# A decoder layer in split fp32: 69 to 73 seven-product k-pairs, and 50 of them with two weight sums made by accumulating DMAs

## The chip, the cores and the metric

The kernel runs on one core of one Trainium2 chip. The metric is the device time of one launch in microseconds (us), as the median of the runs. A core has a matrix engine (TensorE, PE in the profile, with its weight loads as PEld), VectorE (DVE), ScalarE (ACT), GpSimd (POOL), SyncE (SP, which issues most DMAs here) and 16 DMA engines. SBUF is the on-chip memory, PSUM holds the accumulators of PE, and the weights come from DRAM.

## The reference

One layer of a decoder on 256 tokens of width 2048, all in float32. Its work is some thirty products of a 256-row activation with a weight matrix:

```python
hn = rmsnorm(h, norm_mix_w)
q, k, v, g_ret, xr, yr, g_a, g_b = split(hn @ w_in)          # 2048 x 14336
ret_out = silu(g_ret) * groupnorm(retention(rotary(q), rotary(k), v))
rnn_out = gelu(yr) * rg_lru(causal_dwconv(xr))
merged = sigmoid(g_a) * (ret_out @ w_proj_ret) + sigmoid(g_b) * (rnn_out @ w_proj_rnn)
h = h + merged @ w_mix_out
h = h + memory_cross_attention(rmsnorm(h), rmsnorm(mem), xa_w_q, xa_w_k, xa_w_v, xa_w_o)
up = causal_dwconv(rmsnorm(h) @ ffn_w_up)                    # 2048 x 11264
h = h + (silu(gate) * value) @ ffn_w_down                    # 5632 x 2048
return rmsnorm(h, final_norm_w)
```

## The kernel before

**Split products.** Every fp32 operand is split into a high part `hi` (a cast to float32r by ACT, line 446) and a rest `lo` (operand minus `hi`, by DVE, line 447). A product is three matmuls, `hi·hi`, `lo·hi` and `hi·lo` (`mm`, line 280), each 128 x 128 weights by 128 x 512 columns.

**The stream of weights.** `weight_plan` lists the 58 products in their order, and `weight_stream` cuts them into 358 chunks, which stand in DRAM in this order as `wall`. A chunk of a *pair* is one k-pair: two k-tiles of 128 rows by two column blocks of 512, four 128 x 512 tiles, 1 MB. `prefetch` (called by `chunks`) issues a chunk's load on SP, into one of three `raw` buffers, and its splits, two chunks ahead of PE; `hi` and `lo` tiles of 128 x 1024 rotate through six buffers each (`PART_BUFS`). The work that a chunk doesn't feed directly (convolutions, norms, transposes, token sums) is put in between by `later`, with distances in chunks that stand in the table `LAG`. The order on each engine is then made by a scheduler from these.

**Eight products or seven.** A plain k-pair multiplies two token halves by two k-tiles by two column blocks: eight products, 24 matmuls. A *seven-product* k-pair (`steps_pair`, the branch `if k2 in seven`) uses Strassen's scheme in Winograd's form on the 2 x 2 blocks: seven products, 21 matmuls. For it, seven weight tiles are split in place of four, and four weight sums are made first: `seven_parts` (line 468) makes them on DVE, with one add of 128 x 1024 and two of 128 x 512. Sums of the activations come from `sums_of`.

**Sums by DMA.** In the *loaded* kind, `load_twice` fetches one weight tile twice into the buffer `tw` (SP, 512 KB), `add_to` adds two other tiles to it straight from DRAM (POOL queue, line 325, 512 KB, `accum_op=ADD`), and `seven_loaded` (line 332) is left with two DVE adds of 128 x 512; its `raw` load is 768 KB. The *far* kind takes a subtraction from DVE: `request` fetches the weights early as `fr`, `subtract` writes their negative, rounded to float32r, with ACT (line 314), and a DMA on the POOL queue adds the weights themselves to it, which leaves the rest, `fl`; the `hi` cast of such weights is line 340.

**What sets kinds and places.** `MARKS` has one entry for each pair: `3` makes k-pair 3 a seven-product one, `23` a loaded one, `-4` makes k-pair 4 a plain one whose two halves are far, `-14` one with its first half far. `LAG` has the distances of early work, in chunks ahead of the chunk that needs it: `sum_load` and `sum_add` for the two DMAs of the loaded kind, `far_load` and `far` for `request` and `subtract`. `tw`, `fr` and `fl` take slots of the pool `bp`, 31 buffers of 4 KB a partition that also holds activations. The results of `ffn_w_down` are added to the residual rows by DMAs on the POOL queue (`nat<-o`, line 1302).

Of the kernel before, what the change touches and what calls it, by code (L numbers as in the profile page):

```python
# [28 lines left out]
BW = 512  # L29
KC = 4  # L30
KH = 2
# [3 lines left out]
WARM = 7  # L35
FREE = 300
LAG = dict(
    sums=3, two_heads=2, recur=3, gelu=6, merged=4, memory=1, memory_step=4, rnn=0, rnn_step=2,
    heads=6, heads_step=1, squares=4, squares_step=2, rows=17, rows_step=2, residual=2, gate=2,
    value=4, merge_turn=1, query_turn=2, key_turn=3, turn=3, attend=3, acc_m=0, acc_h=0,  # L40
    by_rotate=0, by_conv=0, by_gelu=1, by_attend=0, far=2, far_load=2, sum_load=4, sum_add=4,
)
EPS = 1e-6
GN_EPS = 1e-5
FF_PARTS = [4, 4, 3]
EARLY = [2, 2, 4, 4, 4]
MARKS = [
# [9 lines left out]
]  # L57

O_Q, O_K, O_V, O_G = 0, 1024, 2048, 4096
# [22 lines left out]
def both(w, c, row=0, nk=NT, apart=BW):  # L82

    return w, row, nk, (c, c + apart)


def weight_plan():

    plan = []
    for g in range(2):  # L90
        keys = [("w_in", 0, NT, c + g * BW) for c in (O_Q, O_K)]
        values = [("w_in", 0, NT, O_V + b * BW) for b in range(2)]
        first = [keys[0], values[0], both("w_in", O_K, apart=O_V + BW - O_K)]
        plan += keys + [both("w_in", O_V + 1024)] if g else first
        plan.append(both("w_in", O_G + g * 1024))
    for b in range(4):
        plan += [("w_in", 0, NT, c + b * BW) for c in (O_XR, O_YR)]
    plan += [("w_in", 0, NT, O_GB + b * BW) for b in range(2)] + [both("w_proj_rnn", 0)]
    plan += [both("w_in", O_GB + 1024), both("w_proj_rnn", 1024)]
    plan += [both(w, c + b * BW) for w, c in (("w_in", O_GA), ("w_proj_ret", 0)) for b in (0, 2)]  # L100
    plan += [both("w_mix_out", b * BW) for b in (0, 2)]
    plan += [both("xa_w_k", 0), both("xa_w_q", 0), both("xa_w_q", 2 * BW), both("xa_w_k", 2 * BW)]
    plan += [both(w, b * BW) for w in ("xa_w_v", "xa_w_o") for b in (0, 2)]
    for kind, *a in ff_plan():
        if kind == "down" and sum(a) < NF // 4:
            plan += [both("ffn_w_down", b * BW, a[0] * BW, 4 * a[1]) for b in (0, 2)]
        elif kind == "down":
            plan += [("ffn_w_down", a[0] * BW, 4 * a[1], b * BW) for b in range(4)]
        else:
            plan.append(both("ffn_w_up", a[0] * BW, apart=FF))  # L110
    marks, out = iter(one for stage in MARKS for one in stage), []
    for w, row, nk, c in plan:
        if isinstance(c, tuple):
            one = next(marks)
            seven, far = tuple(k % 10 for k in one if k > 0), tuple(-k for k in one if k < 0)
            loaded = tuple(k % 10 for k in one if k > 10)
            out += [(w, row, nk, (*c, seven, far, loaded))] if seven else [(w, row, nk, half) for half in c]
        else:
            out.append((w, row, nk, c))
    return out  # L120


def marks_of(w, row=0):

    return next((c[2] for one, r, _, c in weight_plan() if (one, r) == (w, row) and isinstance(c, tuple)), ())
# [19 lines left out]

def pieces(i, nk, c):

    sizes = EARLY if i < 2 else [KH] * (nk // KH) if isinstance(c, tuple) else [KC] * (nk // KC)
    return [(sum(sizes[:j]), n) for j, n in enumerate(sizes)]


def in_turn(products):

    return [c for o in products for c in o[:-1]] + [o[-1] for o in products]


def kind_of(c, k):

    if not isinstance(c, tuple):
        return c  # L160
    k2 = k // KH
    kinds = (k2 in c[4], k2 in c[2], k2 in c[3], k2 + 10 in c[3], True)
    return (*c[:2], (4, 1, 2, 3, 0)[kinds.index(True)])


def weight_stream():

    out = [
        [(w, row + k * P, n, kind_of(c, k)) for k, n in pieces(i, nk, c)]
        for i, (w, row, nk, c) in enumerate(weight_plan())  # L170
    ]
    out[:2] = [[one for pair in zip(*out[:2]) for one in pair]]
    out[-4:-1] = [in_turn(out[-4:-1])]
    return [one for chunks in out for one in chunks]


# [18 lines left out]
def hybrid_layer(  # L195
# [17 lines left out]
    act, dve, pe, pool, sp = nc.scalar, nc.vector, nc.tensor, nc.gpsimd, nc.sync  # L213
# [21 lines left out]
    def acc():  # L235
        return pm.tile([P, 2, BW], F32, tag="acc", name=nm("acc"))
# [46 lines left out]
    plan = weight_plan()  # L283
# [9 lines left out]
    at, scale0, split, far = [0], [], [], {}  # L293
# [202 lines left out]
    def ended(steps):  # L496

        for a in steps:
            pass
        return a  # L500
# [34 lines left out]
    def gemm_n(*args):  # L535
        return ended(steps_n(*args))
# [384 lines left out]
    for g in range(2):  # L921
        dec = big([P, 4, S], s="dec")
        vs, turned = [], ([], [])
        for b, o in enumerate((O_Q, O_K)):
# [6 lines left out]
            if b and not g and paired():  # L931
                a, v = pair("w_in", 0, xs, NT, O_K, O_V + BW)
                scaled(a, rs0)
                by_dma(a, rotate_both)
            else:
                a = gemm_n("w_in", 0, xs, NT, o + g * BW) if g + b else q0
                turned_rows(a, rs0, rotate_both, 2 - b if g + b else 3, g + b > 0, LAG["by_rotate"])
            if b == 1:
                sp.dma_start(
                    out=dec,  # L940
# [47 lines left out]
    rnn = []  # L988
# [91 lines left out]
    merged, rsms, hrow = [], [], []  # L1080
# [222 lines left out]

    def down_final(b0, hid, n):

        steps = [steps_n("ffn_w_down", b0 * BW, hid, n, b * BW) for b in range(3)]
        for st in steps:
            for _ in range(n // KC - 1):
                next(st)
        for b, st in enumerate(steps):  # L1310
            h = hrow[b]
            dve.tensor_add(h, h, ended(st))
            finish(b)
        last_down(b0, hid, n, 3)
# [55 lines left out]
    def finish(b):  # L1370

        for tt in range(2):
            y = hrow[b][:, tt, :]
            square(y, ss3[:, tt, b : b + 1])
            dve.tensor_tensor(out=y, in0=y, in1=wfin[b // 2][:, b % 2, :], op=ALU.mult)
# [30 lines left out]
    hid = {}  # L1406
    for kind, b, *n in ff_plan():
        if kind == "up":
            b0 = max(one[1] for one in ff_plan() if one[0] == "down" and one[1] <= b)
            used = marks_of("ffn_w_down", b0 * BW) if b0 < sum(FF_PARTS[:2]) else ()  # L1410
            seven = tuple(i - 2 * (b - b0) for i in used)
            up(b, hid.setdefault(b, []), seven, LAG["value"] if b < NF // 4 - 1 else 3)
        else:
            final = b + n[0] == NF // 4
            if final:
                wfin = []
                for i in range(2):
                    t = big([P, 2, BW], s="wf")
                    sp.dma_start(
                        out=t.rearrange("p a n -> p (a n)"),  # L1420
                        in_=final_norm_w[i * 1024 : (i + 1) * 1024].partition_broadcast(P),
                    )
                    wfin.append(t)
            (down_final if final else down)(b, Hidden(hid, b), 4 * n[0])
# [38 lines left out]
```

## Time and profile before

| | us |
|---|---|
| runs | 1957.58, 1960.05, 1960.06 |
| median | 1960.05 |
| the profiled execution's own time | 1958.17 |
| its span, first to last instruction | 1956.4 |
| PE busy in the span | 1945.4 |
| DVE busy | 1670.9 |
| ACT busy | 1444.6 |
| POOL busy | 49.3 |

The profile is of one execution. Busy time is the time in which an engine had an instruction in work; matmuls overlap, so the busy time of PE says whether it ran, not how fast. A group of instructions is shown by line, engine, operation and tiles, with its count, its busy time, the mean of one, and the idle time ahead of it with what ended it. The chain of waits is followed back from the last instruction. A row of the timeline has the start, the time taken, the instruction, and in brackets the idle time before it. Rows on stretches (windows) give the busy time of each engine in a stretch, the granted clock, the share of time in which the 16 DMA engines were busy, and what they moved.

### The profile page before, as it was taken

How to read it: one execution, taken by the hardware profiler on the slowest of the kernel's cores; microseconds unless marked ns; L12 is line 12 of the kernel's file. 1: busy time of each engine (PE TensorE's matmuls, PEld its weight loads, DVE VectorE, ACT ScalarE, POOL GpSimd, SP SyncE). 2: the span in 40 equal slices, each digit the busy share in tenths (PEclk: the TensorE clock that was granted, in tenths of full speed). 3: DMA queues.
4: the chain of work that ended last, by engine and by line, in shares of the span. 5: the costliest groups of instructions: out<-in, count | busy, mean ns of one | idle time of the engine just before them, and what ended most of it. 6: DMA issues, size and time to landing. Idle time of an engine off the chain costs nothing.

```text
span 1956.4 us, 24194 instructions
## 1 busy us (share of the span) xinstructions
PE 1945.4 (99%) x8747; PEld 1616.2 (83%) x8747; DVE 1670.9 (85%) x2160; ACT 1444.6 (74%) x1774; POOL 49.3 (3%) x48
## 2 busy tenths in 40 slices
PE   9999999999999999999999999999999999999998
PEld 7888888888888888888888888888888888888887
DVE  6897986788999898887888767889999989999986
ACT  6666758999655676778678777888887578874784
POOL 0000000010000000000000000000000000000000
PEclk9999999999999999999999999999999999999999
DMA  8757667766567576778766666676677667768673
GB/s 331 239 202 203 221 227 206 223 209 211 180 226 250 183 269 215 268 241 263 237 212 219 213 190 192 210 253 224 212 231 230 239 223 233 231 198 264 228 234 130
DMA packets 202456, 438.74 MB, mean 224 GB/s; under 512 B 142560, under 2 KB 147168, under 8 KB 158560
## 3 DMA queue, kind: packets, MB, share of 16 engines
q1 hardware_dynamic: 199024, 425.14, 65.3%
q0 software_dynamic: 3312, 12.06, 3.2%
q8 instruction: 68, 1.11, 0.2%
q14 instruction: 52, 0.43, 0.1%
HBM read 391.54 MB, written 2.10 MB: 201 GB/s over the span
## 4 chain that ended last, share of the span: by engine, by line
PE 88%; DVE 6%; ACT 2%; issue 2%; DMA 2%; POOL 0%; SPq 0%; POOLq 0%; DVEq 0%; ACTq 0%
PE acc L280 62%; PE sm L280 26%; DVE lo L447 2%; DMA raw<-in_wall 1%; ACT hi L446 1%; DVE fv L1277 1%; DVE o L622 0%; DVE raw L468 0%; ACT f L672 0%; DVE o L633 0%; DVE s L697 0%; DVE fo L1286 0%; DVE fg L1277 0%; ACT pl L659 0%; ACT fg L1275 0%
## 5 line engine op out<-in xcount | busy, mean ns | idle before, releaser
L447 DVE TENSOR_TENSOR lo<-raw,hi 128x1024 fp32r<-128x1024 f32 (+1 forms) x837 | 963.1, 1178 | 192.4 <-ACT hi L446 185.0
L280 PE MATMUL acc<-hi,s 128*128 128x512 f32 (+1 forms) x3534 | 1083.7, 388 | 1.9 <-ACT hi L446 0.8
L446 ACT CAST hi<-raw 128x1024 fp32r<-128x1024 f32 (+1 forms) x837 | 816.6, 1010 | 327.0 <-DVE raw L468 86.3
L280 PEld LDWEIGHTS acc<-hi,s 128*128 128x128 f32 x3534 | 660.9, 188 | 137.6 <-ACT hi L446 1.3
L280 PE MATMUL acc<-lo,s 128*128 128x512 f32 (+1 forms) x1743 | 676.2, 388 | 0.0
L280 PE MATMUL sm<-hi,s 128*128 128x512 f32 x1496 | 460.9, 389 | 0.0
L280 PEld LDWEIGHTS acc<-lo,s 128*128 128x128 f32 x1743 | 327.5, 188 | 68.2 <-DVE lo L447 1.3
L280 PEld LDWEIGHTS sm<-hi,s 128*128 128x128 f32 x1496 | 280.9, 188 | 58.2 <-ACT prob L1198 0.2
L280 PE MATMUL sm<-lo,s 128*128 128x512 f32 x728 | 283.6, 390 | 0.2 <-DVE lo L447 0.2
L672 ACT COPY f<-pt 128x1024 uint16<-128x1024 uint16 x128 | 167.2, 1354 | 12.2 <-DMA pt<-pl 12.2
L468 DVE TENSOR_TENSOR raw<-raw 128x512 f32<-128x512 f32 (+1 forms) x195 | 169.0, 867 | 2.6
L280 PEld LDWEIGHTS sm<-lo,s 128*128 128x128 f32 x728 | 136.7, 188 | 29.1 <-DVE lo L447 0.8
L280 PE MATMUL acc<-hi,ts 128*128 128x512 f32 x414 | 127.5, 389 | 0.0
L280 PEld LDWEIGHTS acc<-hi,ts 128*128 128x128 f32 x414 | 77.8, 188 | 16.1
L280 PE MATMUL acc<-lo,ts 128*128 128x512 f32 x207 | 80.8, 391 | 0.7 <-DVE lo L447 0.7
L659 ACT COPY pl<-o 128x1024 uint16<-128x1024 uint16 x64 | 62.7, 1040 | 2.9 <-DVE o L633 2.8
L659 ACT COPY pl<-rows 128x1024 uint16<-128x1024 uint16 x44 | 43.8, 1043 | 16.2 <-DVE rows L689 16.2
L1403 ACT ACTIVATE o<-o,ro 128x512 f32<-128x512 f32 x44 | 30.3, 718 | 31.1 <-DVE o L633 30.9
L633 DVE TENSOR_TENSOR o<-o,sm 128x512 f32<-128x512 f32 x64 | 42.6, 684 | 5.6 <-PE sm L280 5.5
L280 PEld LDWEIGHTS acc<-lo,ts 128*128 128x128 f32 x207 | 38.9, 188 | 9.5 <-DVE lo L447 1.5
L1277 DVE SCALAR_TENSOR_TENSOR fg<-f,pf,fg 128x255 f32<-128x255 f32 (+1 forms) x88 | 40.3, 480 | 4.6 <-ACT fg L1275 4.1
L622 DVE TENSOR_TENSOR o<-o,acc 128x512 f32<-128x512 f32 x64 | 43.7, 683 | 0.5
(197 smaller groups left out, 1196.2 us busy)
## 6 DMA issues: line engine op xcount, KB each, us to landing
raw<-in_wall SPq DMA_DIRECT2D x342, 1024.0 KB, 4.9
fr<-in_wall SPq DMA_DIRECT2D x11, 512.0 KB, 6.5
fl<-fr POOLq DMA_DIRECT2D x11, 512.0 KB, 9.0
raw<-in_wall SPq DMA_DIRECT2D x8, 512.0 KB, 7.3
nat<-in_x SPq DMA_DIRECT2D x8, 512.0 KB, 9.9
nat<-o POOLq DMA_DIRECT2D x8, 512.0 KB, 6.6
raw<-in_wall SPq DMA_DIRECT2D x4, 768.0 KB, 4.3
pt<-pl SPq DMA_TRANSPOSE x128, 3.5
```

The costliest lines, as they stand in the source:

```text
L280: tc.keep_in_program_order(pe.matmul(*a, **k))
L446: act.copy(hi[:, cs], src[:, cs])
L447: dve.tensor_tensor(out=lo[:, cs], in0=src[:, cs], in1=hi[:, cs].bitcast(F32), op=ALU.subtract)
L468: dve.tensor_tensor(out=o, in0=a, in1=b, op=ALU.add)
L622: dve.tensor_tensor(out=o, in0=a, in1=b, op=op)
L633: dve.tensor_tensor(out=o, in0=o, in1=a, op=ALU.add)
L659: act.copy(planes[:, tt], words[:, tt])
L672: act.copy(halves_[:, :, :, cs], turned_[:, :, :, cs])
L1277: dve.scalar_tensor_tensor(out=y[:, s:S], in0=z[:, j, 0 : S - s], scalar=pf[:, 2 - s, t : t + 1], in1=y[:, s:S], op0=ALU.mult, op1=ALU.add,)
L1403: act.mul(a[:, tt, :], a[:, tt, :], rs2[:, tt : tt + 1])
```

## The change

It rewrites two tables. `MARKS` now has 73 seven-product k-pairs for 69, and 50 of them are loaded for 4; the twelve halves that are far stood at eleven. All 32 seven-product k-pairs of the feed-forward (31 before) are loaded, where two were. The four that are new are in the second pair of the `w_in` columns of `g_a`, in the first pairs of `xa_w_v` and `xa_w_o`, and in the seventh block of `ffn_w_up`. `LAG` moves some of the early work: the accumulating DMA of a loaded k-pair is issued, in program order, with its chunk (`sum_add` 4 to 0), the negation and DMA of a far one with its chunk too (`far` 2 to 0), and a few tasks shift by one to four chunks (`two_heads`, `rnn`, `heads`, `squares`, `residual`). `by_attend` gives eight scalings of 128 x 512 to ACT that DVE did. The code for a paired last product of `ffn_w_down` (`down_final`, `weight_stream`) is new too, but with `()` as the last mark that product stays as it was, so the new branch isn't taken; the last line of the diff, in the loop over the feed-forward, changes nothing with it.

```diff
 LAG = dict(
-    sums=3, two_heads=2, recur=3, gelu=6, merged=4, memory=1, memory_step=4, rnn=0, rnn_step=2,
-    heads=6, heads_step=1, squares=4, squares_step=2, rows=17, rows_step=2, residual=2, gate=2,
+    sums=3, two_heads=3, recur=3, gelu=6, merged=4, memory=1, memory_step=4, rnn=2, rnn_step=2,
+    heads=2, heads_step=1, squares=2, squares_step=1, rows=17, rows_step=2, residual=5, gate=2,
...
-    by_rotate=0, by_conv=0, by_gelu=1, by_attend=0, far=2, far_load=2, sum_load=4, sum_add=4,
+    by_rotate=0, by_conv=0, by_gelu=1, by_attend=1, far=0, far_load=3, sum_load=4, sum_add=0,
...
-    ((2, 4), (2, 5, -1), (3,), (2, 5), (2, 5), (5, 22), (4, 5),),
+    ((22, 24), (22, 25, -1), (23,), (22, 25), (22, 25), (25, 22), (24, 25),),
...
-    ((2, 3, 4, 6), (2, 5),),
+    ((22, 23, 24, 26), (22, 24), (), (),),
```

What it moves is seen in the order of the instructions. On PE, the program has 8742 instructions before and 8730 now. The first place is on DVE, in the second pair of the first `ffn_w_down`, at its k-pairs 4 and 5, which are seven-product ones that follow each other. `lo` is the rest that line 447 makes (452 in the changed kernel), `raw` the loaded weights, `tw` the twice loaded tile with its sums. Before:

```order
L447 TENSOR_TENSOR lo_12811<-raw_12808,hi_12810 128x1024
L557 TENSOR_TENSOR ts_12777<-tq_12778,ts_12777 128x512
L468 TENSOR_TENSOR raw_12808<-raw_12808 128x1024
L447 TENSOR_TENSOR lo_12815<-raw_12808,hi_12814 128x512
L468 TENSOR_TENSOR raw_12808<-raw_12808 128x512 x2
L447 TENSOR_TENSOR lo_12822<-raw_12808,hi_12821 128x1024
L447 TENSOR_TENSOR lo_12826<-raw_12808,hi_12825 128x1024
L447 TENSOR_TENSOR lo_12856<-raw_12853,hi_12855 128x1024
L468 TENSOR_TENSOR raw_12853<-raw_12853 128x1024
L447 TENSOR_TENSOR lo_12860<-raw_12853,hi_12859 128x512
L468 TENSOR_TENSOR raw_12853<-raw_12853 128x512 x2
L447 TENSOR_TENSOR lo_12867<-raw_12853,hi_12866 128x1024
```

The same place in the changed kernel:

```order
L452 TENSOR_TENSOR lo_12906<-raw_12903,hi_12905 128x1024
L562 TENSOR_TENSOR ts_12871<-tq_12872,ts_12871 128x512
L337 TENSOR_TENSOR raw_12903<-tw_12745,raw_12903 128x512
L452 TENSOR_TENSOR lo_12910<-raw_12903,hi_12909 128x512
L337 TENSOR_TENSOR raw_12903<-raw_12903 128x512
L452 TENSOR_TENSOR lo_12916<-tw_12745,hi_12915 128x1024
L452 TENSOR_TENSOR lo_12920<-raw_12903,hi_12919 128x1024
L452 TENSOR_TENSOR lo_12951<-raw_12948,hi_12950 128x1024
L337 TENSOR_TENSOR raw_12948<-tw_12781,raw_12948 128x512
L452 TENSOR_TENSOR lo_12955<-raw_12948,hi_12954 128x512
L337 TENSOR_TENSOR raw_12948<-raw_12948 128x512
L452 TENSOR_TENSOR lo_12961<-tw_12781,hi_12960 128x1024
```

The add of 128 x 1024 is gone from each of the two k-pairs, and the subtractions from `tw` need the accumulating DMA. The second place is on POOL, around the same product: `nat<-o` adds the first pair's results to the residual, `tw` are the accumulating DMAs. Before:

```order
L315 DMA fl_10775<-fr_10770 128x1024
L325 DMA tw_12189<-in_wall 128x1024
L1302 DMA nat_6990<-o_12636 128x1024
L1302 DMA nat_6896<-o_12635 128x1024
L1302 DMA nat_7137<-o_12963 128x1024
```

And on POOL in the changed kernel:

```order
L330 DMA tw_12414<-in_wall 128x1024
L1307 DMA nat_7025<-o_12726 128x1024
L1307 DMA nat_6931<-o_12725 128x1024
L330 DMA tw_12745<-in_wall 128x1024
L330 DMA tw_12781<-in_wall 128x1024
L330 DMA tw_12992<-in_wall 128x1024
```

The DMAs that fill `tw_12745` and `tw_12781` for the two k-pairs above now stand behind two DMAs that wait for the first pair's results. The third place is on ACT, in the first pair of `w_proj_rnn`, whose k-pair 1 has become a far one (first half). `fr` are its weights, line 345 casts them, line 319 writes the negative that the DMA on POOL adds to. Before, in the nearest far chunk (in the pair of `w_in` behind it):

```order
L314 ACTIVATE fl_4756<-fr_4752 128x1024
L446 CAST hi_4716<-raw_4710 128x1024
L314 ACTIVATE fl_4759<-fr_4754 128x1024
L446 CAST hi_4764<-raw_4762 128x1024
L446 CAST hi_4768<-raw_4762 128x512
L446 CAST hi_4775<-raw_4762 128x1024
L556 CAST ts_4785<-tq_4786 128x512
L446 CAST hi_4779<-raw_4762 128x1024
L446 CAST hi_4818<-raw_4816 128x1024
L446 CAST hi_4822<-raw_4816 128x1024
L340 CAST hi_4850<-fr_4752 128x1024
```

And the new far chunk on ACT in the changed kernel:

```order
L345 CAST hi_4399<-fr_4263 128x1024
L451 CAST hi_4403<-raw_4401 128x1024
L561 CAST ts_4389<-tq_4390 128x512
L319 ACTIVATE fl_4396<-fr_4263 128x1024
L451 CAST hi_4441<-raw_4439 128x1024
```

The negation that stood ten rows ahead of the cast of the same weights now stands three rows behind it.

More of the change, by code (lines that the diff above doesn't have):

```diff
@@ L107, in weight_plan @@
         elif kind == "down":
-            plan += [("ffn_w_down", a[0] * BW, 4 * a[1], b * BW) for b in range(4)]
+            plan.append(both("ffn_w_down", 0, a[0] * BW, 4 * a[1]))
+            plan += [("ffn_w_down", a[0] * BW, 4 * a[1], b * BW) for b in (2, 3)]
         else:
@@ L172, in weight_stream @@
     out[:2] = [[one for pair in zip(*out[:2]) for one in pair]]
-    out[-4:-1] = [in_turn(out[-4:-1])]
+    if isinstance(weight_plan()[-3][3], tuple):
+        two, one = out[-3:-1]
+        out[-3:-1] = [two[:-2] + one[:-1] + two[-2:] + one[-1:]]
+    else:
+        out[-4:-1] = [in_turn(out[-4:-1])]
     return [one for chunks in out for one in chunks]
@@ L1304, in down_final @@
     def down_final(b0, hid, n):
-        steps = [steps_n("ffn_w_down", b0 * BW, hid, n, b * BW) for b in range(3)]
+        row = b0 * BW
+        if paired():
+            two, one = steps_pair("ffn_w_down", row, hid, n, 0, BW), steps_n("ffn_w_down", row, hid, n, 2 * BW)
+            for st, left in ((two, n // KH - 2), (one, n // KC - 1)):
+                for _ in range(left):
+                    next(st)
+            for b, z in enumerate(ended(two)):
+                dve.tensor_add(hrow[b], hrow[b], z)
+                finish(b)
+            dve.tensor_add(hrow[2], hrow[2], ended(one))
+            finish(2)
+            last_down(b0, hid, n, 3)
+            return
+        steps = [steps_n("ffn_w_down", row, hid, n, b * BW) for b in range(3)]
         for st in steps:
@@ L1409, in hybrid_layer @@
             b0 = max(one[1] for one in ff_plan() if one[0] == "down" and one[1] <= b)
-            used = marks_of("ffn_w_down", b0 * BW) if b0 < sum(FF_PARTS[:2]) else ()
+            used = marks_of("ffn_w_down", b0 * BW)
             seven = tuple(i - 2 * (b - b0) for i in used)
```

13 rows, old and new, of the table MARKS are left out of this document.

## The prediction

> **What bounds the kernel now.** I read the page first (busy times, then the chain that ended last), next that chain in order of time for the pace of PE, and then the few places where PE waits.
>
> ```profile
> span 1956.4 us, 24194 instructions
> ...
> PE 1945.4 (99%) x8747; PEld 1616.2 (83%) x8747; DVE 1670.9 (85%) x2160; ACT 1444.6 (74%) x1774; POOL 49.3 (3%) x48
> ...
> PE   9999999999999999999999999999999999999998
> ...
> DVE  6897986788999898887888767889999989999986
> ...
> PE 88%; DVE 6%; ACT 2%; issue 2%; DMA 2%; POOL 0%; SPq 0%; POOLq 0%; DVEq 0%; ACTq 0%
> ```
>
> PE is at work in every slice and carries 88% of the chain. Whether it runs at its own pace is told by one long piece of the chain (start, length, what, count):
>
> ```profile
> 1202.60 48.96 PE acc L280 x216
> ```
>
> 216 matmuls of 512 columns in 48.96 us: one each 0.2267 us. At this pace (half of it for the few with 256 columns) the 8700 matmuls fill the span, so **the count of matmuls times 0.2267 us is the time**, plus PE's waits. Those are short. The largest behind the start-up, in the timeline (start, time, instruction, idle time with what ended it):
>
> ```profile
> 209.85 0.61 PE L280 MATMUL sm<-hi,s 128*128 128x512 f32 x2
> 210.72 0.50 PE L280 MATMUL sm<-lo,s 128*128 128x512 f32 x1 [0.24 <-DVE lo L447]
> ...
> 1502.36 0.61 PE L280 MATMUL acc<-hi,s 128*128 128x512 f32 x2
> 1502.94 0.50 PE L280 MATMUL acc<-lo,s 128*128 128x512 f32 x1
> ...
> 1531.18 0.61 PE L280 MATMUL acc<-hi,ts 128*128 128x512 f32 x2
> 1532.07 0.50 PE L280 MATMUL acc<-lo,ts 128*128 128x512 f32 x1 [0.27 <-DVE lo L447]
> ...
> 1770.47 0.61 PE L280 MATMUL acc<-hi,ts 128*128 128x512 f32 x2
> 1771.48 0.50 PE L280 MATMUL acc<-lo,ts 128*128 128x512 f32 x1 [0.39 <-DVE lo L447]
> ...
> 1915.77 0.39 PE L280 MATMUL acc<-lo,s 128*128 128x512 f32 x1
> ...
> 1916.70 0.50 PE L280 MATMUL acc<-hi,s 128*128 128x512 f32 x1 [0.55 <-ACT s L696]
> ...
> 1917.42 0.50 PE L280 MATMUL acc<-hi,s 128*128 128x512 f32 x1 [0.22 <-DVE s L697]
> ```
>
> Two matmuls should be followed 0.45 us later. It takes 0.87 at 210, 0.58 at 1502, 0.89 at 1531 and 1.01 at 1770: lost are 0.42, 0.13, 0.44 and 0.56, all to a `lo` of DVE. At 1916, two steps of 0.93 and 0.72 stand for 0.23 each: 1.2 us, lost to the last activations. Together 2.7 us; PE can win its count and about this, no more.
>
> **What is removed from PE.** A seven-product k-pair has 21 matmuls for 24. Four more of them make 12 fewer (8742 to 8730 instructions in PE's order): 12 x 0.2267 = **-2.7 us**, straight on the path.
>
> **What DVE gains.**
>
> ```profile
> L468 DVE TENSOR_TENSOR raw<-raw 128x512 f32<-128x512 f32 (+1 forms) x195 | 169.0, 867 | 2.6
> ...
> L332 DVE TENSOR_TENSOR raw<-raw 128x512 f32<-128x512 f32 x4 | 2.8, 691 | 0.1
> L332 DVE TENSOR_TENSOR raw<-tw,raw 128x512 f32<-128x512 f32 x4 | 2.8, 690 | 0.0
> ```
>
> A k-pair's three adds on line 468 cost 169.0 / 65 = 2.60 us of DVE, a loaded one's two 1.38; each k-pair that becomes loaded takes 1.22 us from DVE. All adds before: 169.0 + 4 x 1.38 = 174.5; after: 23 x 2.60 + 50 x 1.38 = 128.8. DVE goes down by some 45 us of 1671. As PE is the bound, none of this is time by itself. It counts where PE waited for DVE: at 1502, 1531 and 1770, all at `ffn_w_down` products whose k-pairs become loaded. At 1770 DVE works without a pause from one of the adds to the late `lo`:
>
> ```profile
> 1764.77 1.22 DVE L468 TENSOR_TENSOR raw<-raw 128x1024 f32<-128x1024 f32 x1
> ...
> 1770.20 3.50 DVE L447 TENSOR_TENSOR lo<-raw,hi 128x1024 fp32r<-128x1024 f32 x3 [0.21 <-ACT hi L446]
> ```
>
> That add goes: a lead of 1.22 us against a lateness of 0.56, so this wait should go. At 1531 two such adds go from the run of work shown in the change, against 0.44; but what started that run late was a load:
>
> ```profile
> 1509.89 8.17 DMA raw<-in_wall
> ...
> 1518.16 1.05 ACT L446 CAST hi<-raw 128x1024 fp32r<-128x1024 f32 x1 [5.68 <-DMA raw<-in_wall]
> ...
> 1506.23 0.86 POOL L1302 DMA_DIRECT2D nat<-o  x1 [62.01 <-DVE o L633]
> 1509.33 0.87 POOL L1302 DMA_DIRECT2D nat<-o  x1 [2.25 <-issue]
> ```
>
> The first row is the chain: this load took 8.17 us where the median (below) is 4.9, with the accumulating DMAs of `nat` issued just ahead of it, and ACT stood 5.68 us for it. The change puts two more accumulating DMAs, of `tw_12745` and `tw_12781`, right behind these two. They land in time themselves: issue at 1510.2 and 6.8 us to land make 1517, where the cast of the sums comes some 3 us behind the cast at 1518. But they can make `raw` later by as much again, 3.3 us, against the 2.4 us that DVE wins. So of the 1.1 us of waits at these three places I take **-0.6** as won, the one at 1770; the bounds are -1.1 and +1.
>
> **What the loaded sums cost the DMA engines.**
>
> ```profile
> q1 hardware_dynamic: 199024, 425.14, 65.3%
> q0 software_dynamic: 3312, 12.06, 3.2%
> ...
> raw<-in_wall SPq DMA_DIRECT2D x342, 1024.0 KB, 4.9
> ...
> tw<-in_wall SPq DMA_DIRECT2D x4, 512.0 KB, 5.9
> tw<-in_wall POOLq DMA_DIRECT2D x4, 512.0 KB, 6.8
> ```
>
> Columns: packets, MB and share of the 16 engines; then KB each and us to landing. The software queue's 23 DMAs (8 `nat`, 11 `fl`, 4 `tw`) take 3.2% of 1956.4 us, 2.7 us of all engines each; the other queue takes 1277 us for 425 MB, 3.0 us a MB. A loaded k-pair adds an accumulating DMA (2.7) and a twofold load of 0.52 MB (1.6) and saves a quarter of `raw` (0.8): 3.5 us. 46 of them are 161 us, 8% of the span, where the engines had 69% to do. On the mean that is hidden; the dense places are the question (last columns: DMA share and GB/s):
>
> ```profile
> 0.00:50.00 50.00, 47.85 (x206) 39.08 (x207) 32.66 (x56) 34.15 (x51) 1.97 (x8) 1.00 0.87 328
> ...
> 1799.00:1840.00 41.00, 41.00 (x182) 33.97 (x181) 38.45 (x42) 23.09 (x26) 1.66 (x2) 1.00 0.66 226
> 1840.00:1882.00 42.00, 42.00 (x187) 34.77 (x187) 39.12 (x53) 37.06 (x46) 0.00 (x0) 1.00 0.65 202
> ```
>
> From 1799 on four k-pairs of one product become loaded: 0.66 x 41 + 4 x 3.5 = 41.1 us of engine work in 41 us, full to the brim by shares. By bytes it is 226 + 4 x 0.79 MB / 41 us = 303 GB/s, below the 328 that the first 50 us moved at a share of 0.87. The next stretch, with two, has room (0.65 x 42 + 7 = 34 of 42), and the `tw` loads and adds are asked for chunks ahead, so that they can spread. I cost this at nothing; the bounds are nothing and the overflow rival below.
>
> The page DMA: Bandwidth & Descriptors of the Trainium skill (Specifications) gives 435 GB/s as the ceiling of the fabric and some 358 as a core's share of DRAM. By it the stretch is not full at 303 and nothing is added, while by the shares it would be up to a us late; the first row's 328 at 0.87 lies nearer to the page.
>
> **What they cost POOL.**
>
> ```profile
> L325 POOL DMA_DIRECT2D tw<-in_wall x4 | 3.7, 934 | 453.4 <-DVE fg L1277 158.3 <-ACT f L672 143.8 <-ACT hi L446 130.7
> ```
>
> 46 issues of 0.93 us are 43 us on an engine that works 49 of 1956: nothing. The page SBUF — State Buffer of the Trainium skill (Who interferes with whom) warns against such DMAs: DVE's copies, casts and scalings in a two-port mode keep POOL from writing descriptors, its two-input adds don't. By the row, issues stay at 0.93 us with DVE busy 85% of the time, mostly in two-input adds; no lockout shows, and the sum would be the same with one of a us at each issue, since POOL idles.
>
> **What the moved far work costs.**
>
> ```profile
> L314 ACT ACTIVATE fl<-fr 128x1024 fp32r<-128x1024 f32 x11 | 11.5, 1054 | 1.3 <-DMA fr<-in_wall 1.3
> ...
> L340 ACT CAST hi<-fr 128x1024 fp32r<-128x1024 f32 x11 | 11.2, 1047 | 3.3 <-PE sm L280 3.3
> ...
> L556 ACT CAST ts<-tq 128x512 fp32r<-128x512 f32 x11 | 6.8, 619 | 4.1 <-DVE tq L554 4.1
> ...
> DMA to landing us min/median/max: 4.7/9.0/12.9
> ```
>
> The last row is the DMA of `fl`. In `w_proj_rnn` the negation now stands three rows behind its cast, and the cast just ahead of it needs a buffer that PE frees, by PE's order, 51 matmuls before the first use of `fl`: 11.6 us. A cast, the token sum's cast and the negation take 1.05 + 0.62 + 1.05, which leaves 8.9 us; the DMA takes 4.7 to 12.9. PE waits 0 to 4 us there; I take the median with a hand-over of 0.3, **+0.4**. The next tightest far k-pair, counted in the same way, has 13.6 us, the rest 16 and more: nothing, with a us as the upper bound.
>
> **Sum.** -2.7 - 0.6 + 0.4 = **-2.9 us** on the profiled execution's 1958.17: 1955.3. That execution lies 1.9 us under the median of 1960.05, and the runs spread over 2.5; I put the shift on the middle of the two, 1959.1: **1956.2**. It is -0.15%, inside 0.2% (3.9 us), which is about what a measurement of this kernel can tell from no change.
>
> **Rivals.**
>
> *The waits go too* (0.35). If the loads aren't delayed, DVE's lead clears 210, 1502 and 1531 with 1770 (1.6 us), part of 1916, and the far DMA is early: -2.7 - 1.6 - 0.5 = -4.8, 1954.3, and -5.4 at most. For it: DVE and ACT pass work to each other at all five places, and a loaded k-pair's sums wait for no add of DVE. Against: the load at 1509.
>
> *The loads become the bound* (0.24), the slower side. An accumulating DMA beside a `raw` load cost it 3.3 us at 1509. With three `raw` buffers a load can start only when the split of three chunks before is done, so where two or more of these fall on each of several loads, ACT, then PE wait for `raw`. It decides where lateness passes the 3 to 5 us that the splits run ahead of PE; at ten products of the feed-forward with 1 us each beyond it, +10, with -2.7 some 1966. Where an add costs the engines 6 us for 2.7, the stretch from 1799 asks for 0.66 x 41 + 27 = 54 in 41, +13 there alone, and the whole some 1980. For it: ACT's 5.68 us. Against: the loaded k-pairs' own loads are a quarter smaller, and PE lost only 0.44 at 1531.
>
> *The change doesn't do what it says*: excluded by the orders of PE, DVE and POOL, which show it.
>
> **Chances.** The forecast, -5 to -1, has 0.41, a quarter of it beyond the bound. The waits going gives 0.32 of its 0.35 there and the forecast 0.10: faster 0.42. The loads as the bound pass +3.9 in 0.21 of 0.24, and an order that loses a few us elsewhere gives 0.03: slower 0.24. Within: 0.34. The range goes from 1951.5 (-5.4 from the lower base, and the spread of the runs) to 1967, with the worse half of the loads' case outside.
>
> **What would show it.** Right: PE's pitch at 0.227 with 12 matmuls fewer, no idle PE near 1770, DMA near 77%, `raw` still landing in 5 to 6 us. Wrong: `raw` landing in 7 or more with ACT and PE idle behind it in the feed-forward; PE idle by over a us at `fl` in `w_proj_rnn`; accumulating DMAs that hold the engines for over 4 us each.

## The result and the profile after

| | before | changed |
|---|---|---|
| median of the runs, us | 1958.82 | 1973.59 |
| lowest and highest, us | 1955.13, 1960.06 | 1972.73, 1979.94 |
| the profiled execution's own time, us | 1958.17 | 1972.73 |

The ratio of the runs is 1.0084, with a 95% interval of 1.0072 to 1.0096 (the quotient of the two medians is 1.0075): the change makes the kernel slower by 0.8%, some 15 us. The prediction, 1956.2 in 1951.5 to 1967.0, was wrong in sign and in range.

The page of the changed kernel, with the lines that answer to those shown of before:

```profile
span 1971.0 us, 24417 instructions
...
PE 1948.9 (99%) x8735; PEld 1612.1 (82%) x8735; DVE 1627.8 (83%) x2129; ACT 1456.9 (74%) x1792; POOL 90.7 (5%) x95
...
q1 hardware_dynamic: 211968, 437.20, 66.6%
q0 software_dynamic: 10080, 36.70, 10.1%
...
PE 80%; DVE 7%; DMA 5%; ACT 5%; issue 3%; SPq 0%; POOL 0%; POOLq 0%; ACTq 0%; DVEq 0%
...
L330 POOL DMA_DIRECT2D tw<-in_wall x50 | 44.2, 884 | 1098.0 <-DMA tw<-in_wall 326.0
...
raw<-in_wall SPq DMA_DIRECT2D x293, 1024.0 KB, 5.2
raw<-in_wall SPq DMA_DIRECT2D x50, 768.0 KB, 5.3
tw<-in_wall SPq DMA_DIRECT2D x50, 512.0 KB, 8.0
tw<-in_wall POOLq DMA_DIRECT2D x50, 512.0 KB, 7.8
```

PE still shows 99%, and yet its part of the chain has fallen from 88% to 80%; what the chain gained is DMA, from 2% to 5%, ACT and DVE. A busy share of 99% hides 15 us in 1971. The medians at landing hide it as well (`raw` 5.2 us for 4.9). One has to look at the dense stretches. The DMA share there adds up the times of the packets that start in a stretch, over 16 engines, and so can pass 1. Two stretches of the feed-forward, before (columns: stretch, length, busy time of each engine with its instructions, granted clock, DMA share, GB/s):

```profile
1500.00:1560.00 60.00, 59.73 (x263) 48.83 (x262) 55.69 (x64) 28.78 (x32) 3.45 (x4) 1.00 0.71 237
1800.00:1850.00 50.00, 50.00 (x222) 41.45 (x221) 45.54 (x49) 31.40 (x36) 0.89 (x1) 1.00 0.67 213
```

and in the changed kernel:

```profile
1500.00:1560.00 60.00, 56.64 (x246) 45.56 (x245) 47.59 (x57) 26.86 (x30) 7.87 (x9) 1.00 0.92 276
1800.00:1850.00 50.00, 47.63 (x206) 37.70 (x205) 39.74 (x46) 24.60 (x28) 6.10 (x7) 1.00 0.93 286
```

The 16 DMA engines go from 0.7 to 0.92 of their time, and PE works 3.1 us less than before in the first stretch and 2.4 less in the second. The chain of waits names the transfer. In the changed kernel, at the second pair of the first `ffn_w_down` (start, length, what):

```profile
1505.64 7.62 DMA tw<-in_wall
...
1513.95 13.50 DMA tw<-in_wall
...
1528.15 0.70 DVE lo L452
...
1529.67 1.05 ACT hi L451
```

and in the tenth block of `ffn_w_up`:

```profile
1816.63 14.99 DMA raw<-in_wall
...
1831.73 1.05 ACT hi L451
...
1832.81 1.24 DVE lo L452
...
1834.09 2.56 PE acc L285 x10
```

At the first place a twofold load takes 7.6 us and the accumulating DMA behind it 13.5 (median 7.8); for the `lo` and `hi` made of it two steps of PE take 1.4 and 1.3 us. At the second a `raw` load needs 15.0 us, right in the time in which two `nat` adds and two `tw` adds are under way.

Where PE's waits lie: the table adds up, from the trace, by how much each matmul started later than 0.227 us behind the one before it (where that was over 0.245 us), from the first product on. All columns but the first two are experiments, told below.

| us of waits of PE in the profiled execution | before | changed | plain write | full raw | feed-forward by DVE | early loaded | ninth by DVE |
|---|---|---|---|---|---|---|---|
| first pair of `w_proj_rnn` | 0 | 1.7 | 0.4 | 1.2 | 1.2 | 1.0 | 1.0 |
| `ffn_w_up`, fifth block | 0 | 2.4 | 1.6 | 2.9 | 0 | 0 | 0.4 |
| first `ffn_w_down` | 0.8 | 3.7 | 1.8 | 2.9 | 1.1 | 0.6 | 0.9 |
| `ffn_w_up`, sixth to eighth | 0 | 1.1 | 0 | 0 | 1.1 | 0 | 0 |
| `ffn_w_up`, ninth | 0 | 1.9 | 0 | 2.0 | 0.5 | 11.2 | 0.6 |
| second `ffn_w_down` | 0.7 | 1.4 | 1.0 | 5.2 | 3.7 | 0 | 1.3 |
| `ffn_w_up`, tenth and eleventh | 0 | 6.1 | 0 | 1.0 | 0 | 0 | 0 |
| the whole kernel | 5.5 | 21.2 | 7.4 | 19.1 | 10.6 | 15.7 | 7.0 |

From before to the changed kernel the waits grow by 15.7 us, 14.8 of it in the feed-forward. With 12 matmuls fewer (-2.7) and an end that takes 1.2 us longer behind the last matmul this gives 14.2, where the profiled executions lie 14.6 apart.

### The profile page after: what moved, and what is told of

The parts are those of the page before. It is cut to its first block, busy times and chain, and to the rows that moved or that the text cites. A ratio compares the mean times of both kernels' runs of the same rounds, so it can differ in the third digit from the quotient of the medians.

```text
span 1971.0 us, 24417 instructions
## 1 busy us (share of the span) xinstructions
PE 1948.9 (99%) x8735; PEld 1612.1 (82%) x8735; DVE 1627.8 (83%) x2129; ACT 1456.9 (74%) x1792; POOL 90.7 (5%) x95
## 3 DMA queue, kind: packets, MB, share of 16 engines
q1 hardware_dynamic: 211968, 437.20, 66.6%
q0 software_dynamic: 10080, 36.70, 10.1%
## 4 chain that ended last, share of the span: by engine, by line
PE 80%; DVE 7%; DMA 5%; ACT 5%; issue 3%; SPq 0%; POOL 0%; POOLq 0%; ACTq 0%; DVEq 0%
PE acc L285 56%; PE sm L285 24%; DVE lo L452 3%; DMA raw<-in_wall 3%; ACT hi L451 2%; DMA tw<-in_wall 1%; ACT f L677 1%; DVE fv L1282 1%; DMA pt<-pl 1%; ACT pl L664 1%; DVE o L638 1%; DVE o L627 1%; DMA fl<-fr 0%; DVE s L702 0%; ACT o L1421 0%
## 5 line engine op out<-in xcount | busy, mean ns | idle before, releaser
L452 DVE TENSOR_TENSOR lo<-raw,hi 128x1024 fp32r<-128x1024 f32 (+1 forms) x798 | 910.6, 1168 | 226.3 <-ACT hi L451 220.7
L285 PE MATMUL acc<-hi,s 128*128 128x512 f32 x3526 | 1081.7, 388 | 1.5 <-ACT hi L451 0.7
L451 ACT CAST hi<-raw 128x1024 fp32r<-128x1024 f32 (+1 forms) x798 | 775.0, 1006 | 301.6 <-DMA raw<-in_wall 95.1
L285 PE MATMUL acc<-lo,s 128*128 128x512 f32 x1727 | 670.0, 388 | 2.4 <-DVE lo L452 2.4
L285 PE MATMUL sm<-hi,s 128*128 128x512 f32 x1464 | 451.2, 389 | 2.5 <-DVE o L638 2.5
L285 PE MATMUL acc<-hi,ts 128*128 128x512 f32 x438 | 135.3, 390 | 0.6 <-ACT hi L451 0.6
L330 POOL DMA_DIRECT2D tw<-in_wall x50 | 44.2, 884 | 1098.0 <-DMA tw<-in_wall 326.0
L452 DVE TENSOR_TENSOR lo<-tw,hi 128x1024 fp32r<-128x1024 f32 x50 | 61.0, 1220 | 21.2 <-ACT hi L451 20.7
L451 ACT CAST hi<-tw 128x1024 fp32r<-128x1024 f32 x50 | 52.4, 1048 | 17.1 <-PE sm L285 6.7
L473 DVE TENSOR_TENSOR raw<-raw 128x512 f32<-128x512 f32 (+1 forms) x69 | 59.7, 865 | 1.0
L285 PEld LDWEIGHTS acc<-lo,ts 128*128 128x128 f32 x219 | 41.1, 188 | 14.4 <-DVE lo L452 6.1
```

What stands on the lines that cost most here:

```text
L285: tc.keep_in_program_order(pe.matmul(*a, **k))
L330: pool.dma_start(out=far[i], in_=source(i)[:, 0:KH, :], accum_op=ALU.add)
L451: act.copy(hi[:, cs], src[:, cs])
L452: dve.tensor_tensor(out=lo[:, cs], in0=src[:, cs], in1=hi[:, cs].bitcast(F32), op=ALU.subtract)
L473: dve.tensor_tensor(out=o, in0=a, in1=b, op=ALU.add)
```

## The experiments

Two theories at first. **The loads**: accumulating DMAs and twofold loads crowd the DMA engines in the feed-forward, and `raw`, `tw` and `nat` land late. **The table**: the new distances of `LAG` put the engines' work in a worse order. Every ratio is to the kernel before, run on the same chip, with its 95% interval.

### The feed-forward's sums by DVE again

```diff
-    ((22, 24), (22, 25, -1), (23,), (22, 25), (22, 25), (25, 22), (24, 25),),
+    ((2, 4), (2, 5, -1), (3,), (2, 5), (2, 5), (5, 22), (4, 5),),
```

The other two rows likewise; the second keeps one loaded k-pair, as this one does.

> The changed kernel with the loaded kind taken back in the feed-forward alone: 30 of its 32 loaded k-pairs get their sums from DVE again, two stay loaded as before; table LAG, the other products and the 73 seven-product k-pairs stay as changed. Theory 'the loads' (accumulating DMAs and twofold loads crowd the 16 DMA engines in the feed-forward, so that raw, tw and nat land late): the 17 us of new waits of PE in the feed-forward go, the 1.7 us at fl in w_proj_rnn stay: 1955 to 1959. Theory 'the table' (the new distances of LAG put ACT's, DVE's and POOL's work in a worse order): the waits stay, 1968 to 1974.

Measured: 1960.28, ratio 1.0002 (0.9991 to 1.0012). The loss is gone. The time is 1.3 us over the range of 'the loads', on a chip where before itself took 1960.23. The second `ffn_w_down` waits 3.7 us (table); the chain ahead of that wait is of DVE's and ACT's own work, with no DMA in it.

### Before, with the feed-forward loaded and nothing else

```diff
-    ((2, 4), (2, 5, -1), (3,), (2, 5), (2, 5), (5, 22), (4, 5),),
+    ((22, 24), (22, 25, -1), (23,), (22, 25), (22, 25), (25, 22), (24, 25),),
```

> The kernel before with one thing of the change: all 31 seven-product k-pairs of the feed-forward loaded (2 before). Its table LAG is the old one, with the accumulating DMA asked for four chunks ahead. 'The loads': 12 to 18 us over before, 1971 to 1977, raw landing in 7 to 15 us from 1505 to 1550 and from 1810 to 1845. 'The table': within 2 us of before, 1957 to 1961.

Measured: 1978.76, 1.0087 (1.0067 to 1.0107). This one part alone makes the whole loss.

### The changed kernel with the old table

```diff
-    by_rotate=0, by_conv=0, by_gelu=1, by_attend=1, far=0, far_load=3, sum_load=4, sum_add=0,
+    by_rotate=0, by_conv=0, by_gelu=1, by_attend=0, far=2, far_load=2, sum_load=4, sum_add=4,
```

and the rows above it.

> The changed kernel with the whole table LAG of before (sum_add 4, far 2, residual 2 and so on). 'The loads': only the 1.7 us at fl and a little of the late adds come back, 1968 to 1973. 'The table': 1955 to 1959.

Measured: 1978.49, 1.0081 (1.0051 to 1.0110): nothing comes back. The table isn't the cause, and asking for the add earlier (`sum_add` 4) doesn't help.

### A plain write in place of the accumulating DMA

```diff
-        pool.dma_start(out=far[i], in_=source(i)[:, 0:KH, :], accum_op=ALU.add)
+        pool.dma_start(out=far[i], in_=source(i)[:, 0:KH, :])
```

> The changed kernel with the DMA of the loaded kind writing its 512 KB over tw in place of adding to it, so that the first two weight sums lack their addend; transfers, bytes from DRAM, waits and order stay. If the price of accumulating on the DMA engines (2.8 us of all 16 for 512 KB, where 512 KB of a plain load take 1.6) is what crowds them, 50 times 1.2 us of engine time go and with them a third to two thirds of the loss: 1961 to 1968. If the count of transfers and their waits for each other matter and not this price, or if 'the table' holds: 1971 to 1974.

Measured: 1960.89, 1.0004 (0.9992 to 1.0016), more than I expected back. Order, buffers, waits and bytes are the same, and the loss is gone: it doesn't go by bytes or by the count of transfers. The rows of its page, and the two stretches:

```profile
q1 hardware_dynamic: 211968, 437.20, 67.4%
q0 software_dynamic: 10080, 36.70, 6.7%
...
tw<-in_wall POOLq DMA_DIRECT2D x50, 512.0 KB, 5.9
```

```profile
1500.00:1560.00 60.00, 59.09 (x259) 48.23 (x259) 50.51 (x58) 28.47 (x33) 6.74 (x10) 1.00 0.92 306
1800.00:1850.00 50.00, 50.00 (x223) 41.40 (x222) 41.33 (x46) 32.37 (x38) 1.98 (x3) 1.00 0.78 267
```

In the changed kernel q0's 70 accumulating DMAs take 10.1% of 1971.0 us, 2.84 us of all 16 engines each. Here 20 are left (56.9 us) and q0 has 6.7% of 1956.8 us, so a plain write of the same 512 KB takes (131.1 - 56.9) / 50 = 1.48, if the 20 cost the mean of the 70. Adding costs the engines 1.9 times the plain transfer. In the second stretch the share falls from 0.93 to 0.78. In the first it stays at 0.92, with more bytes moved, and PE stands idle there for 0.9 us where it stood for 3.4 in the changed kernel.

### Fewer twofold loads, more buffers, other transfers

The twofold load replaced by zeros from GpSimd:

```diff
-        load(t, source(i)[:, 3:4, :].to_broadcast([P, KH, BW]), False)
+        pool.memset(t, 0.0)
```

> The changed kernel without the twofold loads: GpSimd sets tw to zero in their place and the accumulating DMA adds to that, so that the sums lack one addend. 1.6 us of all 16 DMA engines go for each of the 50 loaded k-pairs, and the accumulating DMAs stay. 'Full engines': the loss goes as it did with the plain write, which freed 1.4 us for each: 1957 to 1963. 'Accumulating itself' (a DMA that reads and adds holds up the other transfers in a way that its time on the engines doesn't show): at least 1968.

Measured: 1963.39, 1.0024 (1.0011 to 1.0038): most of the loss is gone, not all. From the fifth block of `ffn_w_up` on, PE waits 4.0 us where the changed kernel waits 17.6, although every accumulating DMA is still there. But some 8 us of new waits stand in the first four blocks, where no other of these kernels waits much; their cause was not followed further, and the profiled execution was the slowest of the nine, 5.2 us over their median. In the dense places, then, taking away either the adding or the twofold load is enough: neither alone makes the loss. (With the twofold load the add's wait for it goes too, which this run doesn't tell apart; with the plain write that wait stayed, and the loss went all the same.)

Four `raw` buffers:

```diff
-RAW_BUFS = 3
+RAW_BUFS = 4
...
-    bp = ctx.enter_context(tc.tile_pool(name="bp", bufs=31))
+    bp = ctx.enter_context(tc.tile_pool(name="bp", bufs=29))
```

> The changed kernel with four raw buffers for three (two of the 31 buffers of the pool are given for it). If the loads are only late, because each may start first when the split three chunks before is done, a load that starts a chunk sooner makes good most of it: 1960 to 1966. If the engines are full over tens of us ('full engines'), starting sooner only lengthens the queue: 1970 to 1977.

Measured: 1999.43, 1.0207 (1.0191 to 1.0222), worse than either theory had it. It doesn't answer the question: `tw` itself is late here. In the chain ahead of a wait of 4.7 us the twofold load starts only when PE is done with a piece of work, and the add behind it:

```profile
1795.08 3.03 PE sm L285 x12
...
1798.13 8.03 DMA tw<-in_wall
...
1806.84 10.43 DMA tw<-in_wall
```

I read this as the load waiting for one of the two buffers that the pool gave up; it was not tried apart.

The plain write with other loads beside it:

```diff
+        pool.dma_start(out=spare, in_=source(i)[:, 0:1, 0:384])
...
-                load(raw, source(i)[:, 0:3, :], False)
+                load(raw, source(i), False)
```

> The plain write in place of the accumulating DMA once more (the sums lack an addend), and other plain loads beside it that take up the engine time it frees: 192 KB into a spare tile on the same queue, and raw loads of 1 MB for 768 KB; by the rates so far 1.5 + 0.6 + 0.8 = 2.9 us of all 16 engines for each loaded k-pair, as much as the accumulating DMA takes. 'Full engines': the loss is back, 1969 to 1976. 'Accumulating itself': it stays away, 1957 to 1963.

Measured: 2021.14, 1.0320 (1.0301 to 1.0339). This tells nothing of the feed-forward: the loads into the one spare tile depend on nothing but each other, and were all put into the kernel's first 220 us, where they block GpSimd's queue one by one (PE waits 22.4 us at 55 and 12.2 at 144):

```profile
52.99 2.62 DMA spare<-in_wall
...
55.99 2.67 DMA spare<-in_wall
```

So I made the test again without the spare tile, with the plain write and the `raw` edit alone (column 'full raw'):

> The plain write in place of the accumulating DMA (the sums lack an addend), and raw loads of 1 MB for 768 KB in the loaded k-pairs: of the 1.4 us of all 16 engines that the plain write freed for each, 0.8 us are taken up again, without another transfer or wait. 'Full engines' (only the time on the engines counts): about half of the loss is back, 1963 to 1968. 'Accumulating itself': 1957 to 1962, as with the plain write alone.

Measured: 1968.71, 1.0051 (1.0035 to 1.0066), some 10 us over before and half-way back, with no accumulating `tw` in it. The same stretches in this run:

```profile
1500.00:1560.00 60.00, 58.27 (x255) 47.19 (x254) 50.88 (x61) 28.79 (x32) 6.21 (x9) 1.00 0.93 319
1800.00:1850.00 50.00, 50.00 (x223) 41.39 (x222) 42.56 (x49) 28.09 (x31) 4.45 (x7) 1.00 0.92 332
```

The engines are as busy as in the changed kernel, now at 319 and 332 GB/s. PE stands idle for 1.7 us in the first stretch, for 3.4 in the changed kernel, and not at all in the second. So a share over 0.9 doesn't by itself cost PE time. The kernel before shows this too, with a share over 1 and PE at work throughout:

```profile
895.00:935.00 40.00, 40.00 (x178) 33.17 (x177) 29.82 (x43) 35.75 (x46) 1.61 (x2) 1.00 1.01 275
```

The `raw` loads issued there landed in 5.5 to 7.4 us. In the changed kernel those issued from 1790 to 1840 took 7.0 to 15.0, where before they took 4.7 to 5.5. What counts is how late the loads get, and whether the splits run far enough ahead of PE. Against the plain write alone the waits grow by 11.7 us (table, 7.4 to 19.1); 6.2 of it stand in the ninth block and the second `ffn_w_down`, next to a second cause that the coming runs show: the chain ahead of this run's longest wait (3.0 us between two starts, at 1738) goes through a DMA transpose, with a plain `tw` write issued 0.3 us behind it:

```profile
1726.69 12.13 DMA pt<-pl
```

So about half of the difference is left for the engines' load. That bytes aren't the measure is shown by the plain write; **time on the engines** agrees with these runs better than bytes do, but is argued and not proven by them.

### One loaded k-pair in each product

```diff
-    ((22, 24), (22, 25, -1), (23,), (22, 25), (22, 25), (25, 22), (24, 25),),
+    ((2, 24), (2, 25, -1), (23,), (2, 25), (2, 25), (5, 22), (4, 5),),
```

The other two rows likewise.

> The changed kernel with 13 of the feed-forward's 32 seven-product k-pairs loaded for 32, one in each product at most. 'Full engines' (a stretch loses time only where raw, tw and nat together ask for more than the DMA engines can move, at a share of about 0.92): with one a product no stretch is full, 1956 to 1960, and DVE is a little less tight than with sums by DVE everywhere. 'Each one costs' (every loaded k-pair delays its neighbours by the same): 13/32 of 15 us, 1964 to 1968.

Measured: 1966.76, 1.0039 (1.0028 to 1.0051). That fits 'each one costs', and I was wrong here: the DMA share is 0.77 and 0.84 in the two stretches, and time is lost all the same, elsewhere: 6.9 us in the ninth block of `ffn_w_up`, 2.7 in the fifth, where the DMA transposes (`pt<-pl`, four at the start of each block) run. So I moved the loaded k-pair in the blocks of `ffn_w_up`:

```diff
-    ((2, 24), (2, 25, -1), (23,), (2, 25), (2, 25), (5, 22), (4, 5),),
+    ((22, 4), (22, 5, -1), (23,), (22, 5), (22, 5), (5, 22), (4, 5),),
```

The other two rows likewise.

> One loaded k-pair in each product of the feed-forward again, as in the run with 13, but in the blocks of ffn_w_up an early k-pair (2, in one block 4) and not the last, 11 in all (one of them in a down product). A tw load is asked for six chunks of PE's time ahead of its use, so for a late k-pair it and its add fell on the transposes of the block's start (issue 1418 and 1424, transposes at 1425 to 1434); for an early one they fall in the second half of the product before. 'Collision' (the adds cost time where they meet the transposes or the nat adds, within 10 us): the waits of 2.7 us in the fifth block and 6.9 us in the ninth go, 1956 to 1960. 'Each one costs': 11/32 of 15 us, 1963 to 1966.

(Loaded are 13, and not 11: 11 in the blocks and 2 in the down products.) Measured: 1961.77, 1.0017 (1.0007 to 1.0026). The fifth block's wait is gone as expected; the ninth's has grown to 11.2 us. The guess was wrong in the ninth block, and the trace says where. SP's and POOL's issues there:

```profile
1674.66 7.62 SPq L665 DMA_TRANSPOSE pt<-pl  x4
1682.39 1.19 SPq L256 DMA_DIRECT2D raw<-in_wall  x2
```

```profile
1677.59 0.87 POOL L330 DMA_DIRECT2D tw<-in_wall  x1 [69.61 <-ACT pl L664]
```

The third transpose was issued at 1677.31, the add 0.28 us later. Both needed 12.6 and 12.5 us, where a transpose's median in this run is 3.3. The stretches around it:

```profile
1670.00:1677.00 7.00, 7.00 (x33) 5.79 (x32) 7.00 (x8) 6.14 (x9) 0.00 (x0) 1.00 0.75 245
1677.00:1690.00 13.00, 13.00 (x59) 10.78 (x58) 5.45 (x10) 6.94 (x9) 0.87 (x1) 1.00 1.19 105
1690.00:1700.00 10.00, 6.46 (x21) 4.22 (x19) 5.62 (x9) 7.05 (x9) 0.86 (x1) 0.83 1.01 361
```

In the middle row the packets fill the engines' time (1.19 of it), and only 105 GB/s are moved. The next `raw` load takes 10.5 us, as the chain says, and PE runs dry at 1690.8:

```profile
1682.39 10.46 DMA raw<-in_wall
```

Is it this meeting? The last two runs take away only that block's loaded k-pair, and then set `far` to 1 as well:

```diff
-    ((3, 22, 4), (22, 5), (22, 4), (24, 5), (5, 22), (4, 2),),
+    ((3, 22, 4), (22, 5), (22, 4), (4, 5), (5, 22), (4, 2),),
```

> The run with eleven early loaded k-pairs in the feed-forward, and one edit: the seven-product k-pairs 4 and 5 of the ninth block of ffn_w_up get their sums from DVE, so that no add is issued beside that block's transposes. 'Meeting' (an add issued within half a us behind a transpose holds both for 12 us): the 11 us lost there go, but for what DVE's sums cost in that place (up to 4): 1951 to 1956. 'Each one costs' or 'full engines' alone: one k-pair less is worth half a us, 1960 to 1962.

> The same with far 1 for 0: the negation in w_proj_rnn a chunk earlier, in front of its cast. If PE's wait of 1.0 to 1.7 us at fl is due to the late negation, another 1 us less than in the run beside it, 1950 to 1955. If the DMA engines set it (three accumulating DMAs land there in 8 to 13 us), no difference.

Measured: 1957.59, 0.9998 (0.9989 to 1.0007), and 1956.19, 0.9995 (0.9986 to 1.0004). One k-pair in 31 takes the ratio from 1.0017 to 0.9998, 3.7 us; between the profiled executions it is 7.9 us (1965.71 to 1957.80), the former being the slowest of its ten runs. So this one k-pair, whose add meets the transposes, makes a loss of its own. That it is the meeting, and not the k-pair's other load, is read from the traces; that its price differs from execution to execution is read from this spread. Neither was tried apart. The same 13 us without the add:

```profile
1677.00:1690.00 13.00, 13.00 (x59) 10.78 (x58) 10.61 (x16) 12.16 (x15) 0.00 (x0) 1.00 1.00 275
```

With `far` 1 the wait of 1.0 us in `w_proj_rnn` is 0; the two ratios differ by 0.0003, which the intervals don't separate.

### The change without the feed-forward

```diff
-    by_rotate=0, by_conv=0, by_gelu=1, by_attend=1, far=0, far_load=3, sum_load=4, sum_add=0,
+    by_rotate=0, by_conv=0, by_gelu=1, by_attend=1, far=1, far_load=3, sum_load=4, sum_add=0,
...
+    ((2, 4), (2, 5, -1), (3,), (2, 5), (2, 5), (5, 22), (4, 5),),
+    ((2, 3, 4), (5,), (2, 4), (2, 5), (5, 22), (2, 4),),
+    ((2, 3, 4, 6), (2, 5), (), (),),
```

The three rows replace the changed kernel's rows of the feed-forward; they are those of before.

> The parts of the change outside the feed-forward alone: its loaded and seven-product k-pairs there, its table LAG (with far 1 for 0); the feed-forward's kinds are those of before. PE has 9 matmuls fewer than before (-2.0 us). 'The loads in the feed-forward are the whole loss': 1954 to 1957 where before is 1958. If the loaded sums outside or the table cost something too: 1959 or more.

Measured: 1956.19, 0.9987 (0.9978 to 0.9996): faster than both kernels, with 18 loaded k-pairs outside the feed-forward and three of the four new seven-product ones. Nine matmuls fewer are 0.9990, so the loaded sums show no cost there.

## Why the prediction was wrong

**The step that failed** is the one on the DMA engines: "On the mean that is hidden; the dense places are the question" and, of these, "I cost this at nothing". Its price per k-pair was right: 2.7 us for an accumulating DMA (2.84 measured), a share of 77% in all (66.6 + 10.1). The stretch from 1799 was found to be "full to the brim by shares", 41.1 us of work in 41. Then I set that aside, because 303 GB/s lay below the 328 that the first 50 us had moved. But bytes don't measure this load, as an add moves its 0.5 MB at half the rate of a plain write: the same share of 0.92 to 0.93 stood for 276 to 286 GB/s in the changed kernel and for 306 to 332 with plain writes. The sum itself came out. In the changed kernel the same 41 us have 1.03 at 307 GB/s, for the 41.1 in 41 and the 303 of the prediction (the tenth block itself runs some 7 us later there; the 41 us from 1806 have 0.91 at 266):

```profile
1799.00:1840.00 41.00, 39.77 (x174) 32.10 (x173) 33.29 (x40) 19.44 (x22) 6.10 (x7) 1.00 1.03 307
```

What failed is that this costs nothing: the `raw` loads landed up to 10 us later than before (above), and the tenth and eleventh blocks lost 6.1 us. By the ceilings of the Trainium skill's page DMA: Bandwidth & Descriptors (Specifications) nothing would be added at 307 GB/s. That is not borne out here, and the measurement decides. I also worked out only that stretch and the next. The first `ffn_w_down`, whose two `nat` adds I had named, went from 237 to 276 GB/s and lost 2.9 us more than before.

**The rival "The loads become the bound"** had the mechanism, its place and its sign, at 0.24. Its size was close: ten products at 1 us for a measured 14.8 us in the feed-forward, and up to 13 us in the stretch from 1799 "alone", where it was 6.1. (The 13 asked for adds of 6 us each on the engines, and they took 2.84.) The range then left out its worse half, in which the result fell.

**The count of matmuls** was right, and so was PE's pace: the changed kernel's chain has

```profile
1201.38 48.96 PE acc L285 x216
```

**DVE** went down by 43 us, forecast 45. The wait at 1770 went, as did the one at 210. The one at 1531, which "can make `raw` later by as much again", became three, and the first `ffn_w_down` waits 3.7 us for 0.8, past my bound of +1. The danger was named, and taken at the value without it.

**POOL**: 44.2 us for 50 issues, 0.88 each, forecast 0.93; no wait of PE is put down to them.

**The far k-pair** was forecast at +0.4, in 0 to 4; it took 1.7. Its chain:

```profile
502.56 0.62 ACT ts L561
503.19 0.97 ACT fl L319
...
504.55 9.39 DMA fl<-fr
...
513.98 1.20 PE acc L285 x4
```

and on ACT's timeline the cast that waits for PE's buffer and the token sum's cast behind it:

```profile
500.99 1.06 ACT L451 CAST hi<-raw 128x1024 fp32r<-128x1024 f32 x1 [0.30 <-PE acc L285]
502.56 0.62 ACT L561 CAST ts<-tq 128x512 fp32r<-128x512 f32 x1 [0.51 <-DVE tq L559]
```

The 51 matmuls, the three pieces of ACT's work and their order were as figured. I had the DMA at 9.0, where it took 9.4, and let the cast, the token sum's cast and the negation follow each other at once. But the token sum's cast waited 0.5 us more for DVE's sums (`tq`), since I took that cast's duration and not what it waits for; the rest, some 0.3 us, went into hand-overs. With the negation a chunk earlier (`far` 1) the wait was 0.

**What was not seen at all** is the meeting of adds and transposes. In the changed kernel two adds were issued 0.7 and 0.4 us behind a transpose, at 1687 and 1728; the slowest transposes beside them took 9.5 and 8.4 us (median 3.5), and the 1.9 and 1.4 us that PE waits in these products stand next to them. How much of that is due to them wasn't tried apart in this kernel.

## What to carry to other kernels

Count a DMA's cost in time on the engines, by its kind, and not in bytes. A stretch of 40 us in which these times add up to over nine tenths is a place to look at: see how late the transfers land there and how far ahead the work runs, since some such stretches cost nothing and others 3 us. Taking work from an engine that isn't the bound (43 us of DVE here) won about 1 us of waits, those at 210 and 1770, and it may cost the resource that it is moved to. Where such sums are loaded, put them where raw loads, transposes and other adds leave room.

## What the runs showed of the hardware

- An accumulating DMA of 512 KB takes 2.84 us of all 16 engines' time (mean of 70, by the packets' times), a plain one on the same queue 1.48.
- A DMA of GpSimd's queue can make a group of DMA transposes late. Over the fifteen profiles 28 were issued inside a group, up to 1.1 us behind one of its transposes or up to 0.3 us ahead of the next. The twelve slowest transposes of all (10.2 to 12.7 us) stand in six of these groups; of the 1676 transposes with no DMA of that queue under way, none took over 9.5, and their median is 3.3. The DMA's own time tells less: eight of the 28 took 9.4 to 12.8 us, but so did many that were issued with no transpose from 3 us ahead of them to 2.5 us behind (147 of 538 `tw` and `spare` DMAs took over 9.3). Thirty were issued up to 2.5 us ahead of a group, and the transposes behind them took 8.5 at most. A plain write is among those in the six groups, so it isn't the adding; what else decides isn't settled. The kernel before has none inside a group.
- After PE has stood for over 2 us, it mostly runs at half its pace for a while. After the wait of 3.2 us in the run with early loaded k-pairs (start, time, instruction):

```profile
1695.90 1.05 PE L285 MATMUL sm<-hi,ts 128*128 128x512 f32 x2
1696.75 0.63 PE L285 MATMUL sm<-lo,ts 128*128 128x512 f32 x1
1697.18 1.00 PE L285 MATMUL acc<-hi,s 128*128 128x512 f32 x2
```

Three matmuls take 1.28 us, 0.427 each for 0.227, and the granted clock of that stretch was 0.83 (above). The same half pace was seen behind 12 of the 13 gaps of 2.1 to 3.3 us between two starts over all runs, in most for five to eight matmuls, at times only after a few at full pace. It wasn't seen behind three gaps of 2.0 or one of 2.9. At 0.2 us each, such a wait mostly costs 1.0 to 1.6 us more than itself. The Trainium skill's page TensorE: Matmul & The Clock Gate (Part 1: The HAM clock gate) puts the return to half rate behind an idle window of about 3.4 us; here it came behind gaps from 2.1 us on.
